# A smaller arena request for the second key tile, a product kept in SBUF, both root spreads ahead of the output, and layer 0's squares in PSUM

## The chip, the cores and the metric

The kernel runs on one core of a Trainium2 chip. The core has five engines with a queue of instructions each, all in order: TensorE (PE; its weight loads are listed as PEld), VectorE (DVE), ScalarE (ACT), GpSimd (POOL) and SyncE (SP), which issues most of the transfers. They wait for one another through semaphores. SBUF is the working memory, 128 partitions wide; PSUM, which TensorE writes to, has eight banks of 512 float32 columns. The metric is the device time of one execution in microseconds, lower is better, compared by medians of several runs.

## What is computed

A decoder trunk of two layers on 512 tokens of width 1024. Each layer normalizes x, projects it for four token mixers (retention, a convolution, a gated DeltaNet and HGRN2), projects their outputs back, and adds a SwiGLU feed-forward part. A last normalization ends it.

```python
D_MODEL, SEQ, DEPTH, D_GROUP, HEAD_DIM, N_HEADS, D_FF = 1024, 512, 2, 256, 64, 4, 2816

for l in range(DEPTH):
    h = rms_norm(x, norm_mix_w[l])
    proj = h @ w_in[l]                                  # 3592 columns
    (rq, rk, rv, rg, ca, cg, gq, gk, gv, gg, gb, ga, hq, hf, hi, hgate) = split(proj)
    ret = head_group_norm(retention_mixer(rq, rk, rv), ret_norm_w[l]) * silu(rg)   # rq, rk are rotated
    conf = conformer_conv_mixer(ca, cg, ...)            # GLU, 31 causal taps, layer norm, swish
    gdn = head_rms_norm(gated_deltanet_mixer(gq, gk, gv, gb, ga, ...), ...) * silu(gg)
    hg = head_rms_norm(hgrn2_mixer(hq, hf, hi, ...), ...) * silu(hgate)
    x = x + concat([ret, conf, gdn, hg]) @ w_out[l]
    h = rms_norm(x, norm_ffn_w[l])
    x = x + (silu(h @ ffn_w_gate[l]) * (h @ ffn_w_up[l])) @ ffn_w_down[l]
return rms_norm(x, final_norm_w)

def rms_norm(x, w, eps=1e-6):
    return x * rsqrt(mean(x * x, axis=-1) + eps) * w
```

## The kernel before

**Layout and number format.** x is kept transposed: eight tiles `x[k]` of 128 channels by 512 tokens. Every float32 operand of a large product is split into a rounded part and the rest (`xh`, `xl`; `whi`, `wlo`), and a product is three matmuls: high by high, low by high, high by low (`mm3`, L461 to L463; for token-major projections L486 to L488). The weights come by DMA into `wraw` (five buffers) and are split by ACT (the cast, L257 or L383) and POOL or DVE (the rest, L258 or L384).

**Order.** The program is written in one order, and the framework lays out each engine's queue from it: an instruction with an earlier place goes first, unless a model of the times says that its inputs or buffers aren't there yet. From then on each queue is fixed. A tile from a pool waits for the release of the buffer that it takes over. Where two instructions touch the same PSUM bank, they are ordered even if they touch different columns.

**PSUM.** The eight banks are two pools of four. `pd` takes the large projections (one bank each, two for token-major ones, `dense_t`, L486 to L488), the input `glu` of the convolution, which is read there by all its taps, and some intermediates of the weight splits. `pm` takes everything else.

**The root mean squares.** `ssq_add` squares one `x[k]` on ACT (L219 for k = 0, straight into `ssq`; L221 into a tile `sq` of a pool of two buffers) and adds it to `ssq` on DVE (L223). `rstd_sum` sums over the channels with matmuls (L231) and takes the reciprocal root on POOL (L213); `rstd_spread` spreads it over the partitions with matmuls (L242) into a `pm` bank, which ACT copies to `rsb` (L246). At the start of layer 0, `split_x` (L251 on ACT, L252 on DVE) and the squares run while x is still arriving, beside POOL's first weight splits.

**The mixers.** `layer` runs the projections in the list `ORDER` (.., ca1, cg1, hgate, rk0, rk1, rq0, rq1, rv, rg). After each projection its evicting function `ev[..]` is emitted. The mixers `gdn`, `hgrn`, `conf` and `ret` are generators; `tick()` moves each active one a step on, after every two slices of a projection. Their SBUF tiles come from an arena of 43 units (`Arena`; tiles of 2 or 4 units, the eight x tiles serve as spare ones of 2). Before an eviction, `ar.can(..)` asks whether the tiles listed in `NEED` for the first two letters of the projection's name can be had; while not, the mixers are ticked. A rotary projection (`ev_rot`) takes two tables `cosr` and `sinr` with rk0 alone (made on POOL, L722 and L723), and two tiles `sw` and `raw` with each of rk0, rk1, rq0 and rq1: ACT copies the swapped halves to `sw` (L727, L728), DVE multiplies the bank by the cosine into `raw` (L729), POOL multiplies `sw` by the sine and adds it (L730, L731). The convolution `conf_taps` runs twice, for two halves of the channels: a first tap (L1288), 23 taps on DVE (L1292), seven on ACT and POOL (L1296, L1298), and a sum (L1302), after which two of its three tiles go back to the arena.

**The feed-forward part.** Beyond its first four columns of tiles it multiplies by a scheme of seven half-width products for each pair (`step`, names e, t1, t2, g, h, t3, t4). It has two banks: `ab` and `cd`, each with a lower and an upper half (`LO`, `UP`) of 256 columns. It is called 26 times per layer, 52 in all. The fourth-named sum is completed late: `end`, with product t4, is put on the list `last`, and runs within the next `step` after its t1. Before the change ACT copies e from cd (L1648), t1 from ab's upper half into cd's upper half (L1650), t2 (L1653) and t3 (L1659, to the tile `u3`); DVE adds the first two sums (L1656) and t3 to cd's upper half (L1660).

**The end.** The last two row tiles of the second layer's down projection are done by token halves. `leave(half)` then spreads the roots of one half, multiplies the eight x tiles by them (k = 1, 4, 7 on POOL from `rsb`, L1696; the others on DVE from the bank, L1698), and issues the output transfers (L1699), even k from ACT's queue, odd k from SP's.

Of the kernel before, what the change touches and what calls it, by code (L numbers as in the profile page):

```python
# [138 lines left out]
def kernel(  # L139
# [72 lines left out]

        GP.tensor_tensor(y, a, mhalf[:, :n], op=ALU.pow)  # L213

    def ssq_add(k, keep=False, c=slice(0, T)):

        sq = sqp.tile([P, T], F32, name="sq")
        if k == 0:
            S.activation(ssq[:, c], x[k][:, c], AF.Square)  # L219
        else:  # L220
            S.activation(sq[:, c], x[k][:, c], AF.Square)  # L221
            if not keep:
                V.tensor_tensor(ssq[:, c], ssq[:, c], sq[:, c], op=ADD)  # L223
        return sq
# [13 lines left out]
    def rstd_spread(blocks=range(NB), half=True):  # L238

        pb = pm.tile([P, T], F32, name="pm")  # L240
        for b in blocks:
            PE.matmul(pb[:, b * P:(b + 1) * P], rst[:, b:b + 1].broadcast_to([P, P]), ident, start=True, stop=True)  # L242
        if half:
            V.tensor_scalar(rsh, rst, 0.5, None, op0=MUL)
        c = slice(blocks[0] * P, (blocks[-1] + 1) * P)
        S.copy(rsb[:, c], pb[:, c])  # L246
        return pb
# [362 lines left out]
    def layer(l, ar, ga, open_mix, gvp, gzp):  # L610
# [796 lines left out]
        def ret_blocks(rk, rq, v, kT, og, pt, scores):  # L1407
            S0 = None
            for b in range(NB):
# [31 lines left out]
                if b % 2 == 1:  # L1441
# [5 lines left out]

        after = {max(("gg", "gv1"), key=ORDER.index): ("gdn", gdn), "hi": ("hgrn", hgrn), "cg1": ("conf", conf), "rv": ("ret", ret)}
        NEED = dict(gg=(4,), hi=(4,), hg=(4,), rv=(4,), rg=(4,), hf=(4, 4, 2, 2), hq=(4,), ca=(2,), cg=(2, 2),
                    rk=(2, 2, 2, 2), rq=(2, 2))  # L1450
        pend = []
        for n, nm in enumerate(ORDER):
            if nm == "gg":
                while not ar.can(*NEED[nm]):
                    tick()
                for ps in dense_t_wide(G + 2 * H):
                    ev_gg(ps)
                continue
            elif nm in T_GROUPS:
                ps = dense_t(G)  # L1460
            elif l == 0 and n < 2:
                if n == 0:
                    first = dense_c2()
                ps = first[n]
            else:

                ps = dense_c(xh, xl, range(KD), pm.tile([P, T], F32, name="pm") if n < 2 else None)
            pend.append((nm, ps))
            if n == R_SUM[l]:
                rstd_sum(range(NB), ssq)  # L1470
            if n < R_SUM[l] + 1:
                continue
            if n == R_SUM[l] + 1:
                rstd_spread()
            for nm, ps in pend:
                while not ar.can(*NEED.get(nm[:2], ())):
                    tick()
                ev[nm](ps)
                if nm in after:
                    q, f = after[nm]  # L1480
                    start(l, q, f())
            pend = []


    for k in range(KD):
        ssq_add(k)
    with tc.tile_pool(name="mload", bufs=1) as mlp:
        mf = mlp.tile([P, 7 * HD], F32, name="mf")
        nc.sync.dma_start(mf, msk)
# [2 lines left out]
    for l in range(DEPTH):  # L1492
# [47 lines left out]
        with tc.tile_pool(name=f"ffp{l}", bufs=1, reuse_waits="tile") as ffp, \  # L1540
# [95 lines left out]
            def step(of, first, second):  # L1636

                def product(ps, nm, start=False):
                    hi, lo = w_next()
                    for k in range(KD // 2):  # L1640
                        mm3(ps, hi, lo, k, *of(k, nm), start and k == 0, k == KD // 2 - 1, True)

                ab = pm.tile([P, T], F32, name="pm")
                cd = pm.tile([P, T], F32, name="pm")
                gs = fft.tile([P, T], F32, name="gs")
                u3 = fft.tile([P, HC], F32, name="u3")
                product(cd[:, LO], "e", True)
                S.copy(gs[:, LO], cd[:, LO])  # L1648
                product(ab[:, UP], "t1", True)
                S.copy(cd[:, UP], ab[:, UP])  # L1650
                finish()
                product(cd[:, LO], "t2")
                S.copy(gs[:, UP], cd[:, LO])  # L1653
                product(ab[:, LO], "g")
                product(ab[:, UP], "h")
                V.tensor_tensor(ab, ab, gs, op=ADD)  # L1656
                first(ab)
                product(cd[:, LO], "t3")
                S.copy(u3, cd[:, LO])  # L1659
                V.tensor_tensor(cd[:, UP], cd[:, UP], u3, op=ADD)  # L1660

                def end():
                    product(cd[:, LO], "t4")
                    second(cd)
                last.append(end)
# [21 lines left out]

                    last.append(lambda: hidden_split(HEAD + PART * (part + 1)))

            def leave(half):  # L1690

                c = slice(half * T // 2, (half + 1) * T // 2)
                pb = rstd_spread(range(2 * half, 2 * half + 2), False)
                for k in range(KD):
                    if k % 3 == 1:
                        GP.tensor_tensor(x[k][:, c], x[k][:, c], rsb[:, c], op=MUL)  # L1696
                    else:
                        V.tensor_tensor(x[k][:, c], x[k][:, c], pb[:, c], op=MUL)  # L1698
                    (nc.sync if k % 2 else nc.scalar).dma_start(out[k * P:(k + 1) * P, c], x[k][:, c])  # L1699

            def down_plain(rows):
                order = plain_order(l, rows)
# [35 lines left out]
            if l + 1 == DEPTH:  # L1738

                rstd_sum(range(NB // 2, NB), ssq, sq)  # L1740
                leave(0)
                leave(1)


def pack(inputs):
# [81 lines left out]
```

## Time and profile before

| what | value |
|---|---|
| median of 3 runs | 1335.5 us (1333.13 to 1335.95) |
| the profiled execution | 1333.43 us |
| its span, first to last instruction | 1331.6 us |
| mean granted TensorE clock | 0.978 |
| weight loads busy (PEld) | 1177.3 us |
| moved by DMA | 124.52 MB, 94 GB/s in the mean |

The profile is of one execution on the chip. Busy times count an engine's instructions, not its waits. A row of a timeline gives start, duration, engine, line, operation, output <- inputs, shapes and count; in brackets how long the engine had been idle before and what it waited for. A row of groups gives the count, the busy time in all and the mean in ns of one, then the idle time before them and what ended it. The granted clock is the share of TensorE's full clock that the throttle let through.

### The profile page before, as it was taken

The numbers are of one execution on the slowest core, as the hardware profiler recorded it, in microseconds if no ns is written. First come the engines' busy times: TensorE is split into PE (matmuls) and PEld (weight loads), VectorE is DVE, ScalarE is ACT, GpSimd is POOL, SyncE is SP. The second block draws the span as 40 slices with busy tenths as digits, with TensorE's granted clock in tenths as the row PEclk, the third lists the DMA queues.
The fourth block names the chain that finished last, engine by engine and source line by source line (L and its number), as shares of the span: only waits on it lengthen the run. The fifth ranks groups of instructions, "written<-read, shape, count | busy, mean of one in ns | idle before, by whom it ended". The sixth has DMA issues, their size and how long they took to land.

```text
span 1331.6 us, 23717 instructions
## 1 busy us (share of the span) xinstructions
PE 1287.8 (97%) x8984; PEld 1177.3 (88%) x8984; DVE 897.5 (67%) x1569; ACT 705.5 (53%) x1454; POOL 788.4 (59%) x669
## 2 busy tenths in 40 slices
PE   8999998899999999999999999999999999999996
PEld 6888887888889999999888889889788999999995
DVE  5753778646787867876465448686559777678645
ACT  5553543535456656655545435445444665566554
POOL 6376773753255765676545767747523666566762
PEclk9999998899999999999999999889999999999998
DMA  7223210134043333342542232002423243333322
GB/s 270 79 79 105 75 25 9 41 111 134 25 135 96 111 112 96 97 126 80 164 138 80 81 88 67 25 1 71 154 69 103 80 123 102 110 97 110 122 78 72
DMA packets 60386, 124.52 MB, mean 94 GB/s; under 512 B 17520, under 2 KB 26992, under 8 KB 60272
## 3 DMA queue, kind: packets, MB, share of 16 engines
q1 hardware_dynamic: 58832, 121.83, 30.0%
q8 instruction: 71, 1.16, 0.4%
q10 hardware_dynamic: 1440, 1.18, 0.3%
q14 instruction: 43, 0.35, 0.1%
HBM read 116.17 MB, written 6.82 MB: 92 GB/s over the span
## 4 chain that ended last, share of the span: by engine, by line
PE 82%; DVE 8%; POOL 5%; ACT 3%; issue 2%; DMA 0%; SPq 0%; POOLq 0%; ACTq 0%; DVEq 0%
PE pm L461 12%; PE pm L462 12%; PE pm L463 12%; PE pd L461 10%; PE pd L462 10%; PE pd L463 10%; PE pd L486 2%; PE pm L1189 2%; PE pd L488 2%; PE pd L487 2%; POOL wlo L258 2%; DVE x L1292 1%; PE pm L928 1%; ACT whi L383 1%; PE pm L1062 1%
## 5 line engine op out<-in xcount | busy, mean ns | idle before, releaser
L258 POOL TENSOR_TENSOR wlo<-wraw,whi 128x512 fp32r<-128x512 f32 (+2 forms) x192 | 248.9, 1305 | 227.3 <-ACT whi L257 186.7
L384 POOL TENSOR_TENSOR wlo<-wraw,whi 128x512 fp32r<-128x512 f32 x208 | 272.5, 1329 | 104.4 <-ACT whi L383 99.9
L461 PE MATMUL pm<-bh,whi 128*128 128x256 f32 x1008 | 282.5, 282 | 3.9 <-ACT pm L1650 2.0
L462 PE MATMUL pm<-bl,whi 128*128 128x256 f32 x1008 | 281.2, 280 | 0.0
L463 PE MATMUL pm<-bh,wlo 128*128 128x256 f32 x1008 | 276.5, 280 | 0.0
L257 ACT CAST whi<-wraw 128x512 fp32r<-128x512 f32 (+2 forms) x212 | 125.3, 598 | 188.1 <-PE pd L462 105.1
L461 PEld LDWEIGHTS pm<-bh,whi 128*128 128x128 f32 x1008 | 189.6, 188 | 6.8 <-DVE pm L1660 3.1
L462 PEld LDWEIGHTS pm<-bl,whi 128*128 128x128 f32 x1008 | 190.0, 188 | 0.5
L463 PEld LDWEIGHTS pm<-bh,wlo 128*128 128x128 f32 x1008 | 187.8, 189 | 0.1
L383 ACT CAST whi<-wraw 128x512 fp32r<-128x512 f32 x208 | 126.7, 624 | 50.1 <-PE pm L462 42.7
L461 PE MATMUL pd<-xh,whi 128*128 128x512 f32 x384 | 151.6, 396 | 0.6 <-DVE x L729 0.6
L463 PE MATMUL pd<-xh,wlo 128*128 128x512 f32 x384 | 151.9, 396 | 0.0
L462 PE MATMUL pd<-xl,whi 128*128 128x512 f32 x384 | 151.6, 396 | 0.0
L384 DVE TENSOR_TENSOR wlo<-pd,whi 128x512 fp32r<-128x512 f32 x156 | 107.3, 688 | 52.4 <-ACT whi L383 49.9
L383 ACT CAST whi<-pd 128x512 fp32r<-128x512 f32 x156 | 92.0, 590 | 64.9 <-PE pm L462 22.6
L378 POOL TENSOR_TENSOR wraw<-wraw 128x512 f32<-128x512 f32 x52 | 68.8, 1324 | 78.2 <-DVE pd L366 65.9
L486 PE MATMUL pd<-whi,xh 128*128 128x256 f32 (+1 forms) x320 | 94.2, 295 | 8.0 <-DVE x L1292 3.4
L487 PE MATMUL pd<-wlo,xh 128*128 128x256 f32 (+1 forms) x320 | 93.7, 293 | 0.0
L488 PE MATMUL pd<-whi,xl 128*128 128x256 f32 (+1 forms) x320 | 93.5, 293 | 0.0
L461 PEld LDWEIGHTS pd<-xh,whi 128*128 128x128 f32 x384 | 72.3, 188 | 16.7 <-DVE x L729 0.8
L462 PEld LDWEIGHTS pd<-xl,whi 128*128 128x128 f32 x384 | 72.2, 188 | 16.0
L463 PEld LDWEIGHTS pd<-xh,wlo 128*128 128x128 f32 x384 | 72.2, 188 | 15.9
(359 smaller groups left out, 3181.0 us busy)
## 6 DMA issues: line engine op xcount, KB each, us to landing
wraw<-in_wf_dram SPq DMA_DIRECT2D x88, 512.0 KB, 3.6
wraw<-in_wc_dram SPq DMA_DIRECT2D x34, 512.0 KB, 3.6
wraw<-in_wd_dram SPq DMA_DIRECT2D x32, 512.0 KB, 4.0
wraw<-in_wt_dram SPq DMA_DIRECT2D x16, 512.0 KB, 3.6
wraw<-in_wo_dram SPq DMA_DIRECT2D x32, 256.0 KB, 2.6
x<-in_xt_dram SPq DMA_DIRECT2D x16, 256.0 KB, 3.7
wraw<-in_wd_dram SPq DMA_DIRECT2D x16, 256.0 KB, 2.7
wraw<-in_wd_dram SPq DMA_DIRECT2D x20, 128.0 KB, 2.0
```

The lines of the kernel that those rows point to most:

```text
L257: S.copy(hi[:, :n], r)
L258: eng.tensor_tensor(lo[:, :n], r, hi[:, :n].bitcast(F32), op=SUB)
L378: GP.tensor_tensor(src, c, a, op=SUB)
L383: S.copy(hi, src)
L384: eng.tensor_tensor(lo, src, hi.bitcast(F32), op=SUB)
L461: PE.matmul(ps, hi[:, w], ah, start=first, stop=False, skip_group_check=shared)
L462: PE.matmul(ps, hi[:, w], al, start=False, stop=False, skip_group_check=shared)
L463: PE.matmul(ps, lo[:, w], ah, start=False, stop=last, skip_group_check=shared)
L486: PE.matmul(o, xh[k][:, tk], hi[:, w], start=(k == 0 and first), stop=False)
L487: PE.matmul(o, xh[k][:, tk], lo[:, w], start=False, stop=False)
L488: PE.matmul(o, xl[k][:, tk], hi[:, w], start=False, stop=(k == KD - 1 and last))
L1189: PE.matmul(ps[:, (bb * 2 + ct) * P:(bb * 2 + ct + 1) * P], k[:, ct * T + b * P:ct * T + (b + 1) * P], qx[:, (ct * NB + b) * P:(ct * NB + ...
```

## The change

There are four edits. In `NEED`, the second key tile rk1 gets an entry of its own, which asks for two tiles of 2 units instead of four. In `step`, ACT copies t1 to an SBUF tile `p5` instead of cd's upper half; cd's upper half is then written once, as the sum of t3, read from cd's lower half, and `p5`; the copy L1659 goes. `leave` spreads both halves' roots before any multiplication, and multiplies the last tile of the second half on DVE instead of POOL. In layer 0's first seven additions of squares, the square goes to a `pd` bank instead of the SBUF tile.

```diff
--- before.py
+++ after.py
@@ -212,9 +212,9 @@
 
         GP.tensor_tensor(y, a, mhalf[:, :n], op=ALU.pow)
 
-    def ssq_add(k, keep=False, c=slice(0, T)):
-
-        sq = sqp.tile([P, T], F32, name="sq")
+    def ssq_add(k, keep=False, c=slice(0, T), bank=False):
+
+        sq = (pd.tile([P, T], F32, name="pd") if bank else sqp.tile([P, T], F32, name="sq")) if k or not bank else None
         if k == 0:
             S.activation(ssq[:, c], x[k][:, c], AF.Square)
         else:
@@ -1447,7 +1447,7 @@
 
         after = {max(("gg", "gv1"), key=ORDER.index): ("gdn", gdn), "hi": ("hgrn", hgrn), "cg1": ("conf", conf), "rv": ("ret", ret)}
         NEED = dict(gg=(4,), hi=(4,), hg=(4,), rv=(4,), rg=(4,), hf=(4, 4, 2, 2), hq=(4,), ca=(2,), cg=(2, 2),
-                    rk=(2, 2, 2, 2), rq=(2, 2))
+                    rk=(2, 2, 2, 2), rk1=(2, 2), rq=(2, 2))
         pend = []
         for n, nm in enumerate(ORDER):
             if nm == "gg":
@@ -1473,7 +1473,7 @@
             if n == R_SUM[l] + 1:
                 rstd_spread()
             for nm, ps in pend:
-                while not ar.can(*NEED.get(nm[:2], ())):
+                while not ar.can(*NEED.get(nm, NEED.get(nm[:2], ()))):
                     tick()
                 ev[nm](ps)
                 if nm in after:
@@ -1483,7 +1483,7 @@
 
 
     for k in range(KD):
-        ssq_add(k)
+        ssq_add(k, bank=True)
     with tc.tile_pool(name="mload", bufs=1) as mlp:
         mf = mlp.tile([P, 7 * HD], F32, name="mf")
         nc.sync.dma_start(mf, msk)
@@ -1643,11 +1643,11 @@
                 ab = pm.tile([P, T], F32, name="pm")
                 cd = pm.tile([P, T], F32, name="pm")
                 gs = fft.tile([P, T], F32, name="gs")
-                u3 = fft.tile([P, HC], F32, name="u3")
+                p5 = fft.tile([P, HC], F32, name="u3")
                 product(cd[:, LO], "e", True)
                 S.copy(gs[:, LO], cd[:, LO])
                 product(ab[:, UP], "t1", True)
-                S.copy(cd[:, UP], ab[:, UP])
+                S.copy(p5, ab[:, UP])
                 finish()
                 product(cd[:, LO], "t2")
                 S.copy(gs[:, UP], cd[:, LO])
@@ -1656,8 +1656,7 @@
                 V.tensor_tensor(ab, ab, gs, op=ADD)
                 first(ab)
                 product(cd[:, LO], "t3")
-                S.copy(u3, cd[:, LO])
-                V.tensor_tensor(cd[:, UP], cd[:, UP], u3, op=ADD)
+                V.tensor_tensor(cd[:, UP], cd[:, LO], p5, op=ADD)
 
                 def end():
                     product(cd[:, LO], "t4")
@@ -1687,16 +1686,17 @@
 
                     last.append(lambda: hidden_split(HEAD + PART * (part + 1)))
 
-            def leave(half):
-
-                c = slice(half * T // 2, (half + 1) * T // 2)
-                pb = rstd_spread(range(2 * half, 2 * half + 2), False)
-                for k in range(KD):
-                    if k % 3 == 1:
-                        GP.tensor_tensor(x[k][:, c], x[k][:, c], rsb[:, c], op=MUL)
-                    else:
-                        V.tensor_tensor(x[k][:, c], x[k][:, c], pb[:, c], op=MUL)
-                    (nc.sync if k % 2 else nc.scalar).dma_start(out[k * P:(k + 1) * P, c], x[k][:, c])
+            def leave():
+
+                pbs = [rstd_spread(range(2 * half, 2 * half + 2), False) for half in range(2)]
+                for half, pb in enumerate(pbs):
+                    c = slice(half * T // 2, (half + 1) * T // 2)
+                    for k in range(KD):
+                        if k % 3 == 1 and (half == 0 or k < KD - 1):
+                            GP.tensor_tensor(x[k][:, c], x[k][:, c], rsb[:, c], op=MUL)
+                        else:
+                            V.tensor_tensor(x[k][:, c], x[k][:, c], pb[:, c], op=MUL)
+                        (nc.sync if k % 2 else nc.scalar).dma_start(out[k * P:(k + 1) * P, c], x[k][:, c])
 
             def down_plain(rows):
                 order = plain_order(l, rows)
@@ -1738,8 +1738,7 @@
             if l + 1 == DEPTH:
 
                 rstd_sum(range(NB // 2, NB), ssq, sq)
-                leave(0)
-                leave(1)
+                leave()
 
 
 def pack(inputs):
```

## The prediction

> **What bounds the kernel now.** First the totals, then stretches of the execution by engine. The columns of a stretch: length, busy time (instructions) of PE, weight loads, DVE, ACT and POOL, granted TensorE clock, DMA share, GB/s.
>
> ```profile
> span 1331.6 us, 23717 instructions
> PE 1287.8 (97%) x8984; PEld 1177.3 (88%) x8984; DVE 897.5 (67%) x1569; ACT 705.5 (53%) x1454; POOL 788.4 (59%) x669
> ...
> 0.00:30.00 30.00, 26.18 (x88) 19.04 (x89) 19.88 (x28) 17.33 (x32) 19.98 (x25) 0.94 0.82 297
> ...
> 450.00:480.00 30.00, 29.91 (x253) 29.71 (x252) 22.43 (x37) 17.44 (x38) 20.11 (x16) 1.00 0.32 103
> ...
> 237.00:266.00 29.00, 28.97 (x225) 28.87 (x227) 18.66 (x31) 16.64 (x32) 24.77 (x25) 0.90 0.15 47
> 200.50:237.00 36.50, 28.19 (x239) 25.54 (x236) 29.94 (x62) 13.44 (x29) 12.55 (x10) 0.89 0.03 8
> 852.90:889.20 36.30, 31.60 (x239) 29.27 (x236) 30.34 (x61) 13.02 (x28) 12.38 (x10) 0.76 0.03 8
> ```
>
> TensorE is the bound: 97% busy, 1331.6 - 1287.8 = 43.8 us idle. Only an edit that removes PE idle time, or lets PE run at a better clock, can move the end. In the feed-forward part (450 to 480) PE idles 0.1 us and the clock is 1.00; 253 matmuls, nearly all of 256 columns, take 29.9 us, so 0.118 us each. The mixers lose far more: between 200.5 and 237 PE idles 36.5 - 28.2 = 8.3 us, and the same place of layer 1 (852.9 to 889.2) idles 4.7 us, both at a lowered clock (0.89, 0.76). These two stretches hold only small matmuls, because no projection can start there. The timelines of the single engines say why (start, us, engine, line, op, out<-in, [idle before <- releaser]):
>
> ```profile
> 176.57 0.58 ACT L727 COPY x<-pd 32x512 f32<-32x512 f32 x1
> ...
> 189.97 1.27 POOL L722 TENSOR_TENSOR x<-cs,rsb 128x512 f32<-128x512 f32 x1
> ...
> 191.71 0.68 DVE L729 TENSOR_TENSOR x<-pd,x 128x512 f32<-128x512 f32 x1
> ...
> 192.82 0.48 PE L461 MATMUL pd<-xh,whi 128*128 128x512 f32 x1
> ...
> 200.14 0.39 PE L463 MATMUL pd<-xh,wlo 128*128 128x512 f32 x1
> ...
> 196.25 0.81 DVE L1288 TENSOR_SCALAR x<-pd,hcw,vc 128x512 f32<-128x512 f32 x1 [2.44 <-POOL x L731]
> ...
> 236.99 0.69 DVE L1302 TENSOR_TENSOR x<-x,x 128x511 f32<-128x511 f32 x1
> 237.72 0.69 DVE L729 TENSOR_TENSOR x<-pd,x 128x512 f32<-128x512 f32 x1
> ...
> 237.03 0.55 PE L486 MATMUL pd<-whi,xh 128*128 128x256 f32 x1 [3.40 <-DVE x L1292]
> ```
>
> L729 is the product that empties a rotary projection's PSUM bank. rk0's runs at 191.71 and hands its bank to rq1's product (192.82 to 200.14). rk1's, whose copies ran from 176.57, comes only at 237.72, right behind L1302, the last step of the convolution's second half (begun at 196.25). Until then the four "pd" banks hold rk1, rq0, rq1 and the convolution's input, and PE's next projection (rv) starts at 237.03 after a wait of 3.40.
>
> **The keys' request.** I followed the arena's lists through the emission order by hand. When rk1 comes, 40 of 43 units are out and one tile of 2 is free. The old request of four tiles needs 40 + 3 x 2 = 46: refused. So the mixers are ticked until the convolution's second half has been emitted and returns two tiles (five ticks), and rk1's product then lands in one of these: that is why L729 follows L1302. The new request of two needs 40 + 2 = 42: granted at once, in a fresh tile. rk1's L729 then waits for its copies (done by about 179) and the cosine table (189.97 + 1.27 = 191.2), and can run behind rk0's, at about 192.4. One bank is free 45 us earlier.
>
> The refusal doesn't vanish: it moves to rq0, where 42 + 2 = 44 is over 43. So rq0 and rq1 keep their banks until 237, as does the convolution's input. What one bank allows is half of rv: 8 slices x 2 token blocks x 3 matmuls = 48 at 0.118 = 5.7 us, which can stand in the idle 8.3 us of layer 0 and in the 4.7 us of layer 1. From 237 to 266 PE is 28.97 of 29 us busy, so what was done before shortens that. The ret mixer starts when rv is out, so it moves along. In the queues: DVE takes rk1's 0.7 us ahead of the convolution's 41 us, and POOL an L731 (1.3 us); both only change places. ACT and POOL must split rv's weights earlier, and POOL is busy 12.55 of 36.5 us there. SP's weight loads follow the splits, in a stretch with a DMA share of 0.03.
>
> Upper end per layer: 5.7, and if the filler also lifts the clock from 0.89 to 1.00, 28.2 x 0.11 = 3.1 more: 9. Lower end: nothing excludes a loss, because all following instructions change places in queues that run in order; the unit of such a loss is the 3.40 us wait above. I take 4 per layer (most of 5.7, since a gap can be too short for a matmul triple): **8 us**, with ends -7 and +18.
>
> **The fifth product.** The same matmul line and two helpers, kept apart by shape, and then two of its stalls:
>
> ```profile
> L461 PE MATMUL pm<-bh,whi 128*128 128x256 f32 x1008 | 282.5, 282 | 3.9 <-ACT pm L1650 2.0 <-DVE pm L1660 1.9
> L461 PEld LDWEIGHTS pm<-bh,whi 128*128 128x128 f32 x1008 | 189.6, 188 | 6.8 <-DVE pm L1660 3.1 <-ACT pm L1650 2.8
> L1659 ACT COPY u<-pm 128x256 f32<-128x256 f32 x52 | 19.3, 371 | 12.4 <-PE pm L463 12.0
> L1650 ACT COPY pm<-pm 128x256 f32<-128x256 f32 x52 | 19.3, 371 | 4.5 <-PE pm L463 4.0
> ...
> 415.89 0.28 PE L463 MATMUL pm<-bh,wlo 128*128 128x256 f32 x1
> ...
> 416.26 0.36 ACT L1650 COPY pm<-pm 128x256 f32<-128x256 f32 x1 [0.20 <-PE pm L463]
> ...
> 416.67 0.39 PE L461 MATMUL pm<-bh,whi 128*128 128x256 f32 x1 [0.50 <-ACT pm L1650]
> ...
> 395.96 0.43 DVE L1660 TENSOR_TENSOR pm<-pm,u 128x256 f32<-128x256 f32 x1 [0.62 <-ACT u L1659]
> ...
> 396.45 0.39 PE L461 MATMUL pm<-bh,whi 128*128 128x256 f32 x1 [0.23 <-DVE pm L1660]
> ```
>
> At 415.89 "t1" ends; the next product, "t2", writes the lower half of the bank cd, and waits because L1650 writes the upper half of that bank. With the copy in an SBUF tile, cd isn't touched, and the wait goes. What is late next: "g" and "h" write the bank that the copy reads, but "t2" (12 x 0.118 = 1.4 us) stands before them and the copy takes 0.37. At 396.45 "t4" waits for the sum L1660, and that for the copy L1659 (0.37 us). Without this copy the sum starts that much sooner and the 0.23 to 0.4 us stalls go. The sum keeps its shape (one PSUM and one SBUF input), so I leave it at 0.43. ACT loses 52 x 0.371 = 19.3 us, which is worth nothing by itself: ACT is busy 53%. The new tile lives two products longer, in two buffers, and a step takes seven products. PE idle 3.9 and weight-load idle 6.8 are the ends of what the stalls cost (a stall shows in either). That they would reappear as waits for weights is possible, so the low end is 0. I take **4.5**.
>
> The Trainium skill speaks against this edit: "Perfetto Trace Analysis", section "Optimizing Scalar/DVE Operations", gives ScalarE about 93 ns of overhead on SBUF against about 51 on PSUM, and by that the t1 copy would take 42 ns more, 2.2 us of ACT in all. The rows disagree: 371 ns into PSUM and 371 into SBUF. By either, ACT has the room.
>
> **The squares.** Sums over DVE rows with both inputs in SBUF (L223) and with one in PSUM (L1714), and the first microseconds:
>
> ```profile
> L223 DVE TENSOR_TENSOR ssq<-ssq,sq 128x512 f32<-128x512 f32 x33 | 32.1, 972 | 0.8 <-ACT sq L221 0.5
> L1714 DVE TENSOR_TENSOR x<-x,pd 128x512 f32<-128x512 f32 x30 | 19.7, 677 | 2.3 <-PE pd L463 2.3
> ...
> 10.34 4.99 POOL L258 TENSOR_TENSOR wlo<-wraw,whi 128x512 fp32r<-128x512 f32 x3 [4.82 <-ACT whi L257]
> ...
> 11.34 1.15 DVE L223 TENSOR_TENSOR ssq<-ssq,sq 128x512 f32<-128x512 f32 x1 [0.54 <-ACT sq L221]
> 12.42 1.75 DVE L252 SCALAR_TENSOR_TENSOR xl<-x,vc,xh 128x512 fp32r<-128x512 f32 x1
> 14.10 1.78 DVE L223 TENSOR_TENSOR ssq<-ssq,sq 128x512 f32<-128x512 f32 x1
> ...
> 20.72 3.47 DVE L223 TENSOR_TENSOR ssq<-ssq,sq 128x512 f32<-128x512 f32 x2
> ...
> 14.23 0.77 PE L462 MATMUL pm<-xl,whi 128*128 128x512 f32 x1 [1.75 <-DVE xl L252]
> ...
> 34.42 1.05 PE L242 MATMUL pm<-cs,rst 128*128 128x128 f32 x8
> ...
> PE pd L486 <- DVE z L674: 2.6, 1, 2.6
> ```
>
> An addition from PSUM takes 677 ns whatever POOL does; one from SBUF alone is stretched to 1.15 to 1.78 while POOL's splits run. The four stretched ones give back 1.15 + 1.78 + 3.47 - 4 x 0.68 = 3.7 us of DVE. The first, at 11.34, stands before the xl on which PE waits 1.75 us: xl could start 0.4 to 0.5 sooner. If it then also ran unstretched (0.75), PE would get 1.4. The Trainium skill's rule limits this: "SBUF — State Buffer", section "Who interferes with whom", has a DVE instruction with two SBUF inputs and a GpSimd read block each other for whole instructions, and xl keeps two, so by it xl still stands out POOL's split, and the gain is about 0.5. I take 0.5 from the start difference alone. Four banks instead of two buffers also end ACT's waits for L223.
>
> A sum that is ready earlier can bring the whole root earlier: spread at 34.42, evictions after it, and at their end PE's 2.6 us wait for z. But PE's place for the spread is fixed when the program is laid out, so from 0 to 2.6; I take 1. The seven squares leave their banks by 24 us, before gg needs them. Together **1.5**, ends 0 and 3.1.
>
> **The end.** ACT's queue and stretches of the last microseconds:
>
> ```profile
> 1321.26 0.37 ACT L246 COPY rsb<-pm 128x256 f32<-128x256 f32 x1 [0.71 <-PE pm L242]
> 1322.12 1.87 ACTq L1699 DMA_DIRECT2D out_dram<-x  x4
> 1324.03 0.37 ACT L246 COPY rsb<-pm 128x256 f32<-128x256 f32 x1 [2.40 <-POOL x L1696]
> ...
> 1324.00:1326.00 2.00, 0.00 (x0) 0.00 (x0) 1.57 (x5) 0.37 (x1) 1.52 (x3) 0.50 1.05 335
> 1326.00:1328.00 2.00, 0.00 (x0) 0.00 (x0) 0.17 (x1) 0.00 (x0) 0.57 (x1) 0.50 0.82 269
> ```
>
> The second copy of the roots stands in ACT's queue behind four output DMAs. Moved ahead of them it runs at about 1323 instead of 1324.03, and the second half's products follow. But the output is bound by its DMAs (335 GB/s, share 1.05), and only the dip to 269 can be won: (1 - 269/335) x 2 = 0.4 us. Against it, ACT's first output DMA now waits for the second copy, about 1 us. **0**, ends -0.9 and +0.4.
>
> **Sum.** 8 + 4.5 + 1.5 + 0 = 14. The profiled execution took 1333.4 (its span 1331.6 and 1.8 around it), 2.1 under the median of 1335.5. 1333.4 - 14 = 1319.4, 1335.5 - 14 = 1321.5; I forecast 1321.
>
> **Rivals.** (A) The wait only moves on: rq0 takes the keys' place, rv's half isn't put forward in PE's order, or what is won before 237 is lost behind 266, where the output projection waits for ret. For: the count above. Against: rq1 did use rk0's bank 0.4 us after it was free. Only 4.5 + 1.5 remain: 1329.5. Chance 0.18. (B) More than half of rv: the freed bank is used again by rg, and the clock recovers: 18 + 6.8 + 3.1 = 28, so 1308. Chance 0.13. (C) Slower: rv's early matmuls stand in PE's queue before the DeltaNet's and wait there for a weight split or the second bank, and each such stop holds a chain that feeds DVE, whose convolution steps free the banks. A stop costs about 3.4 us, as at 237.03. With 6 us won elsewhere it decides from two stops in all; four give 1335.5 - 6 + 13.6 = 1343. Against it: rq1's 24 matmuls ran in that place without one. Chance 0.19, of which 0.12 end slower. The forecast itself has 0.50 (1313 to 1328).
>
> A measurement of this kernel tells some 0.2% (2.7 us) from no change. Faster: 0.50 + 0.13 + 0.15 of A = 0.78; the same: 0.03 of A and 0.07 of C; slower: 0.12. From 1309 to 1337 leaves out half of B and the slow part of C.
>
> **What would show it.** Keys: L729 twice near 192, L486 matmuls on pd between 200 and 237, and PE idle there under 5 us. Fifth: no PE wait on the t1 copy and under 1 us on the sum. Squares: every L223 of the first 25 us near 0.68. End: both copies L246 before 1324, counted from the same point. Wrong would be: pd matmuls still beginning at 237, or new PE waits between 190 and 300.

## The result, and the profile after

| kernel | median, us | runs | ratio to before, 95% interval |
|---|---|---|---|
| before | 1335.07 | 1333.13 to 1335.95 | |
| after | 1305.09 | 1303.31 to 1307.05 | 0.9778 [0.9756, 0.9799] |
| after, measured again beside its variants | 1305.36 | 1302.63 to 1307.67 | 0.9789 [0.9763, 0.9814] |

The forecast was 1321, with a range from 1309. The change took 30.0 us off (1335.07 - 1305.09), where the sum of the terms was 14. The page of the kernel after, its totals and its groups:

```profile
span 1300.1 us, 23700 instructions
...
PE 1268.8 (98%) x8984; PEld 1162.2 (89%) x8984; DVE 883.4 (68%) x1570; ACT 690.8 (53%) x1402; POOL 788.1 (61%) x668
...
L461 PE MATMUL pm<-bh,whi 128*128 128x256 f32 x1008 | 281.1, 281 | 0.0
...
L461 PE MATMUL pd<-xh,whi 128*128 128x512 f32 x384 | 153.2, 400 | 4.3 <-DVE ar L637 4.3
```

Three things are to be seen here. First, the same 8984 matmuls are busy for 1268.8 us instead of 1287.8: 19.0 us less for the same work. Second, PE's idle time fell from 43.8 to 31.3 (1300.1 - 1268.8), 12.5 us. So more than half of the gain is not idle time. Third, the feed-forward matmuls no longer wait (3.9 before, 0.0 now), while a wait of 4.3 us on L637 is new.

The keys, in the timeline of DVE and then of PE, kernel after:

```profile
192.54 0.69 DVE L729 TENSOR_TENSOR x<-pd,x 128x512 f32<-128x512 f32 x1 [1.55 <-POOL x L722]
193.15 0.68 DVE L729 TENSOR_TENSOR ar<-pd,x 128x512 f32<-128x512 f32 x1
...
236.34 0.69 DVE L1302 TENSOR_TENSOR x<-x,x 128x511 f32<-128x511 f32 x1
237.06 0.69 DVE L729 TENSOR_TENSOR x<-pd,x 128x512 f32<-128x512 f32 x1
```

```profile
30.73 1.05 PE L242 MATMUL pm<-cs,rst 128*128 128x128 f32 x8
...
204.00 0.28 PE L486 MATMUL pd<-whi,xh 128*128 128x256 f32 x1
...
214.07 0.28 PE L486 MATMUL pd<-whi,xh 128*128 128x256 f32 x1
236.29 0.38 PE L486 MATMUL pd<-whi,xh 128*128 128x256 f32 x1 [0.26 <-DVE x L1292]
```

Both keys' products run at 192.5 and 193.2; rq0's follows L1302, as the count of the arena had it. Sixteen L486 matmuls, a third of the 48 that make half of rv, run between 204.0 and 214.1, and the next one comes at 236.29. The first row also shows the root's spread 3.7 us earlier than in the kernel before (34.42 to 30.73); how much of this the squares make is taken up below. The stretches of the kernel after that answer to those of the prediction (same columns):

```profile
0.00:30.00 30.00, 26.17 (x97) 19.23 (x98) 14.43 (x28) 17.74 (x33) 19.99 (x26) 0.94 0.83 298
200.50:237.00 36.50, 34.64 (x340) 31.80 (x338) 32.59 (x65) 17.30 (x39) 16.61 (x13) 1.00 0.05 15
237.00:266.00 29.00, 28.70 (x235) 27.20 (x233) 21.03 (x41) 15.77 (x31) 27.78 (x30) 1.00 0.20 65
```

Between 200.5 and 237 PE now idles 1.9 us instead of 8.3, and the granted clock, 0.89 and 0.90 before in the last two stretches, is 1.00 in both. In the first 30 us DVE is busy 14.43 us instead of 19.88. Of these 5.4 us, 3.6 are the seven additions of squares (8.3 us before, 4.7 now) and 1.4 the xl tiles, L252 (7.9 and 6.5). The view of groups by shape has the seven in one row:

```profile
L223 DVE TENSOR_TENSOR ssq<-ssq,pd 128x512 f32<-128x512 f32 x7 | 4.7, 678 | 0.0
```

To see where the gain arises I divided each profiled execution at the first matmul of each root mean square (L231); the differences of these starts are the lengths, in us. The two columns in the middle are kernels of the next section, with the keys' edit alone and with all edits but the squares:

| stretch | before | keys alone | all but the squares | after |
|---|---|---|---|---|
| start to the first root | 25.9 | 24.2 | 24.1 | 22.0 |
| layer 0, mixers | 309.5 | 296.2 | 296.2 | 303.3 |
| layer 0, feed-forward | 342.9 | 343.0 | 337.5 | 337.5 |
| layer 1, mixers | 306.9 | 301.0 | 299.9 | 297.0 |
| layer 1, feed-forward | 333.7 | 333.7 | 328.7 | 328.7 |
| last root to the end | 12.7 | 11.6 | 11.6 | 11.6 |
| span | 1331.6 | 1309.7 | 1298.0 | 1300.1 |

Each column is one execution. The first stretch differs by some 2 us between kernels that are equal up to there (24.0 in one of them). The mixers differ too where the code is the same: over four kernels without the keys and the squares, layer 0 took 309.5 to 312.5 us and layer 1 306.0 to 309.4. So differences of 2 to 3 us in these rows are not read.

### The profile page after: what moved, and what is told of

It reads as the page before. It is cut to its first block, busy times and chain, and to the rows that moved or that the text cites. A ratio compares the mean times of both kernels' runs of the same rounds, so it can differ in the third digit from the quotient of the medians.

```text
span 1300.1 us, 23700 instructions
## 1 busy us (share of the span) xinstructions
PE 1268.8 (98%) x8984; PEld 1162.2 (89%) x8984; DVE 883.4 (68%) x1570; ACT 690.8 (53%) x1402; POOL 788.1 (61%) x668
## 4 chain that ended last, share of the span: by engine, by line
PE 91%; DVE 6%; POOL 1%; ACT 1%; DMA 1%; issue 0%; SPq 0%; DVEq 0%; POOLq 0%; ACTq 0%
PE pm L461 14%; PE pm L462 14%; PE pm L463 14%; PE pd L461 11%; PE pd L463 11%; PE pd L462 11%; PE pd L486 3%; PE pd L488 3%; PE pd L487 3%; PE pm L1189 2%; DVE x L1292 1%; PE pm L928 1%; DVE ar L623 1%; DVE ar L1197 1%; PE pm L1051 1%; PE pm L1036 1%
## 5 line engine op out<-in xcount | busy, mean ns | idle before, releaser
L486 PE MATMUL pd<-whi,xh 128*128 128x256 f32 (+1 forms) x320 | 92.5, 290 | 5.6 <-DVE z L674 3.4
L463 PEld LDWEIGHTS pd<-xh,wlo 128*128 128x128 f32 x384 | 72.7, 189 | 16.3
```

Source lines behind the costliest of these rows:

```text
L463: PE.matmul(ps, lo[:, w], ah, start=False, stop=last, skip_group_check=shared)
L486: PE.matmul(o, xh[k][:, tk], hi[:, w], start=(k == 0 and first), stop=False)
```

## The experiments

### Each edit by itself

Four kernels, each with one edit on the kernel before. **The keys** (one_keys):

```diff
-                    rk=(2, 2, 2, 2), rq=(2, 2))
+                    rk=(2, 2, 2, 2), rk1=(2, 2), rq=(2, 2))
...
-                while not ar.can(*NEED.get(nm[:2], ())):
+                while not ar.can(*NEED.get(nm, NEED.get(nm[:2], ()))):
```

> The kernel before with the keys' entry in NEED alone. Theory 1 (each edit acts at its own place; the sizes are those read from the two traces): some 20 us faster, 10 in each layer's mixer, near 1315. Theory 2 (the sizes forecast): 8 us faster, near 1327. Theory 3 (the edits help one another, the keys' entry needs the others): under 4 us faster.

1312.74 us (1309.57 to 1314.07), ratio 0.9843 [0.9819, 0.9867]: 20.9 us of 1332.65, where my term was 8. The stretch from rq1's first matmul to rg's last holds the same work in both kernels (in layer 0 524 matmuls, in layer 1 521), so it can be compared directly. First two stretches of the kernel before, then the same of the kernel with the keys alone, layer 0 and layer 1:

```profile
192.80:265.40 72.60, 64.26 (x524) 60.08 (x522) 53.46 (x97) 32.68 (x65) 42.77 (x42) 0.91 0.07 23
845.10:915.00 69.90, 65.14 (x521) 61.21 (x521) 52.50 (x97) 32.46 (x65) 42.38 (x40) 0.88 0.07 21
```

```profile
191.10:252.60 61.50, 57.72 (x524) 54.08 (x522) 49.58 (x97) 32.42 (x65) 42.40 (x41) 1.00 0.08 27
833.10:895.10 62.00, 57.39 (x521) 54.04 (x522) 50.69 (x96) 32.10 (x66) 41.74 (x39) 1.00 0.08 24
```

Layer 0 is shorter by 11.1 us: idle time fell from 72.60 - 64.26 = 8.34 to 3.78, which is 4.6, and the busy time of the same 524 matmuls by 6.5, with the clock up from 0.91 to 1.00. Layer 1 is shorter by 7.9, of which 0.15 is idle time (4.76 to 4.61) and 7.75 is busy time (0.88 to 1.00). The gain is 19.0 us here, and 14.3 of it is busy time. Finer windows show that this is the clock: in the kernel before it is 0.50 for 13.7 us of the first stretch and 17.1 us of the second, in which PE is busy for 12.8 and 16.3 us. At full clock half of that would go, 14.6 us. With the keys alone the clock is 1.00 through both stretches. The rest of one_keys' 21.9 us of span adds up from smaller stretches of both signs: 1.7 at the start, 2.2 and 0.9 behind rg, 1.1 at the end, and 2.9 lost in layer 1 ahead of rq1.

**The fifth product** (one_fifth):

```diff
-                u3 = fft.tile([P, HC], F32, name="u3")
+                p5 = fft.tile([P, HC], F32, name="u3")
...
-                S.copy(cd[:, UP], ab[:, UP])
+                S.copy(p5, ab[:, UP])
...
-                S.copy(u3, cd[:, LO])
-                V.tensor_tensor(cd[:, UP], cd[:, UP], u3, op=ADD)
+                V.tensor_tensor(cd[:, UP], cd[:, LO], p5, op=ADD)
```

> The kernel before with the product kept in SBUF and summed from the bank, alone. Theory 1: 10.4 us faster (5.4 in layer 0's feed-forward part, 5.0 in layer 1's), near 1325. Theory 2 (the forecast size): 4.5 us faster. Theory 3: under 4 us.

1321.83 us (1318.30 to 1326.26), ratio 0.9916 [0.9886, 0.9947], 11.2 us; my term was 4.5. The two feed-forward parts of the kernel before, then of one_fifth:

```profile
335.40:678.30 342.90, 339.69 (x2539) 322.76 (x2537) 251.03 (x412) 202.28 (x427) 205.27 (x162) 1.00 0.35 108
985.20:1318.90 333.70, 330.37 (x2525) 316.47 (x2524) 242.02 (x410) 198.93 (x422) 191.75 (x151) 1.00 0.31 94
```

```profile
336.50:674.00 337.50, 337.50 (x2540) 322.53 (x2538) 249.25 (x412) 195.52 (x401) 210.75 (x162) 1.00 0.36 109
983.30:1312.40 329.10, 329.08 (x2526) 316.88 (x2525) 241.88 (x410) 191.76 (x396) 191.57 (x151) 1.00 0.32 95
```

They are shorter by 5.4 and 4.6 us, 10.0 in all. Idle time gives 3.2 + 3.3 = 6.5 of it; the other 3.5 us is busy time at a clock of 1.00 throughout. A stop costs more than its wait, and this is about the size of it. In the prediction's row at 416.67 the first matmul after a wait of 0.50 lasts 0.39 instead of 0.28, and the timeline of PE in the kernel before shows the next one:

```profile
416.90 0.28 PE L462 MATMUL pm<-bl,whi 128*128 128x256 f32 x1
417.01 0.28 PE L463 MATMUL pm<-bh,wlo 128*128 128x256 f32 x1
```

From the last start before the stop (415.89) to 416.90 there are 1.01 us in place of two steps of 0.118: 0.77 lost, where the idle time says 0.50. The list of PE's waits in layer 0's feed-forward part of the kernel before (us in all, times, longest) counts the stops:

```profile
PE pd L461 <- ACT ph L1568: 1.2, 1, 1.2
PE pm L461 <- ACT pm L1650: 1.0, 2, 0.5
PE pm L461 <- DVE pm L1660: 0.9, 3, 0.3
```

Six stops in each layer, twelve in all, at 0.27 more (0.77 - 0.50) make 3.2, near the 3.5. This is an estimate from one stop.

**The squares** (one_squares; `bank=True`, the first and the fourth hunk of the change) and **the end** (one_end; the last two hunks):

```diff
-        sq = sqp.tile([P, T], F32, name="sq")
+        sq = (pd.tile([P, T], F32, name="pd") if bank else sqp.tile([P, T], F32, name="sq")) if k or not bank else None
...
-        ssq_add(k)
+        ssq_add(k, bank=True)
```

> The kernel before with layer 0's squares in PSUM alone. Theory 1: the spread of the roots comes 3.7 us sooner, 1.4 of it is left at 53 us, and the end is 0 to 1.5 us sooner. Theory 2 (the forecast): 1.5 us faster. Theory 3: the early change shifts the whole layer 0 mixer, and the time moves by 3 us or more either way.

```diff
-                leave(0)
-                leave(1)
+                leave()
```

> The kernel before with both roots spread ahead of the products, alone. Theory 1: 1.1 us faster, all after the last projection. Theory 2 (the forecast): no change. What counts is the stretch from the last projection's end to the end of the span.

The squares by themselves: 1332.63 us in ten runs, ratio 0.9995 [0.9973, 1.0018], no difference that can be told. Its profiled execution was the slowest of the ten. In it the first root came at 21.2, against 24.0 to 25.9 in kernels without the edit, and the mixers of layer 0 took 316.9 against 309.5 to 312.5. So something is gained and given back; that is taken up below. The end: 1332.86 us in ten runs, 0.9989 [0.9969, 1.0009]. Its last stretch is 11.7 instead of 12.7, but it is 11.6 with the keys alone, where that edit is absent. So the end has no gain that these runs show.

### Is it the bank, or the order of emission?

The smaller request changes two things: rk1's bank is freed, and the convolution's steps are emitted five ticks later against rk1's eviction. keys_fresh keeps the old request with its five ticks and gives rk1's product a tile of its own:

```diff
-                sw, raw = ar.get(2), ar.get(2)
+                sw = ar.get(2)
+                raw = ar.fresh(2) if (nm, ct) == ("rk", 1) else ar.get(2)
```

> The kernel before, old request, so the five ticks stay, and with them the order in which everything is emitted; but rk1's raw tile is a fresh one (two units over the arena's count), so its product no longer waits for the convolution's end. Theory 1 (the gain comes from the PSUM bank that rk1's product frees): rk1's L729 near 192, 48 matmuls of rv ahead of the convolution's end, and most of the 20 us. Rival (the gain comes from the order: mixers five steps behind the projections): under 5 us, L729 may be early all the same.

1313.81 us (1308.85 to 1316.32), ratio 0.9844 [0.9811, 0.9877], equal to one_keys (0.9843). rk1's product runs at 190.80, behind rk0's at 190.19. The bank that is free earlier is the cause. It is not the ticks.

### Is it the clock?

warm8 adds 112 needless matmuls of 256 columns to the kernel before, in the second half of the convolution of both layers; nothing reads their results. The bank isn't freed earlier than before (rk1's product runs at 243.2; 237.7 before).

```diff
                 if n % CONF_TAPS == CONF_TAPS - 1:
+                    if ct == 1:
+                        pw = pm.tile([P, T], F32, name="pm")
+                        for _ in range(8):
+                            PE.matmul(pw[:, :G], xh[0][:, :P], xl[0][:, :G], start=True, stop=True)
                     yield
```

> The kernel before with 7 times 8 needless matmuls of 256 columns in each second half of the convolution (112 in all; by 0.118 us 13 us of PE work, with nobody reading them). Theory 1 (part of the gain is the granted clock, which PE's idle time between 200 and 237 lowers to 0.89 and 0.76): the clock there rises towards 1.00 and the time doesn't rise, it falls by up to 6 us. Rival (only the useful work that is put forward counts): the clock rises or not, the time stays or rises by up to 13 us.

1327.02 us in nine runs, ratio 0.9952 [0.9936, 0.9968]: 6.4 us faster with more work. One stretch of the kernel before, and the same of warm8:

```profile
190.00:270.00 80.00, 71.40 (x577) 66.66 (x576) 59.51 (x109) 35.63 (x71) 50.00 (x51) 0.91 0.09 27
```

```profile
190.00:270.00 80.00, 75.53 (x651) 70.99 (x652) 60.87 (x113) 37.54 (x74) 51.01 (x50) 0.98 0.09 28
```

In the same 80 us warm8 issues 74 matmuls more, and the clock is 0.98. Over the whole execution PE does 112 matmuls more and is busy 3.7 us less (1287.8 and 1284.1). This profile is of the fastest of the nine runs, but the mean clock is 0.986 to 0.990 in all nine, against 0.976 to 0.981 in the fourteen runs of the kernel before beside them. The new instructions could also have helped by shifting the queues. So the same matmuls were put into a kernel in which that stretch is filled already: all edits but the squares (no_squares, below), with a clock of 1.00 from 180 to 240.

> The 112 needless matmuls of warm8 (in the second half of the convolution of both layers), now put into the kernel without the squares in PSUM, where rv's first half already fills that stretch and the granted clock from 180 to 240 is 1.00. Theory: warm8 gained 0.0048 because the needless matmuls kept the granted clock up where TensorE idled; here nothing is left to recover, so there is no gain, and up to 112 x 0.118 = 13 us of work that now finds little idle time costs something: ratio 0.976 to 0.985, 1302 to 1315. Rival: warm8 gained because the additional instructions changed the order of the queues; then a gain of some 6 us can come here too: 0.971, 1296.

1308.23 us (1306.64 to 1308.85), ratio 0.9807 [0.9790, 0.9823], against 0.9759 [0.9737, 0.9782] without them: there the same work costs 6.4 us (0.0048 of 1334). The mean clock stays where it was (0.991 to 0.993, against 0.989 to 0.994), and PE is busy 13.4 us more (1265.3 and 1278.7), which is the price of 112 matmuls at 0.118 us. Where the clock had dropped, needless matmuls gained; where it hadn't, they cost. The order of the queues also differs between these kernels and may have a share in the 6.4 us of warm8. But that the clock makes up most of the keys' gain is shown by this and by the busy time of the same matmuls above.

### Which copy held the feed-forward part?

t1_sbuf moves only the copy of t1 to SBUF; ACT still copies t3, into a tile of a new pool `ffu` that has one buffer where `u3` had two.

```diff
-                u3 = fft.tile([P, HC], F32, name="u3")
+                p5 = fft.tile([P, HC], F32, name="p5")
+                u3 = ffu.tile([P, HC], F32, name="u3")
...
-                S.copy(cd[:, UP], ab[:, UP])
+                S.copy(p5, ab[:, UP])
...
-                V.tensor_tensor(cd[:, UP], cd[:, UP], u3, op=ADD)
+                V.tensor_tensor(cd[:, UP], p5, u3, op=ADD)
```

> The kernel before with t1 copied to SBUF, but t3 still copied by ACT before the sum. Theory 1: the gaps before t2 go (6.4 us with the slower first matmul after each), those before t4 stay (about 1.3 us), and so does the wait at the end of each feed-forward part (2.7 us): 6 to 7 us faster. Rival (the copy of t3 is what matters, it holds ACT's queue at each step): under 3 us faster.

1326.56 us (1324.80 to 1330.87), ratio 0.9942 [0.9918, 0.9965]. Its two feed-forward parts:

```profile
335.60:676.30 340.70, 339.36 (x2538) 322.71 (x2537) 268.32 (x412) 202.03 (x427) 208.66 (x162) 1.00 0.36 108
982.40:1314.40 332.00, 330.89 (x2525) 317.24 (x2524) 258.29 (x410) 199.60 (x422) 200.59 (x151) 1.00 0.32 94
```

2.2 + 1.7 = 3.9 of the 10.0 us is here. The waits for t1's copy are gone, those for the sum remain (idle 1.34 + 1.11). The wait of 1.2 us for L1568 at the end of each part, which I expected to stay, is gone too. The sum reads both inputs from SBUF here and takes 1.02 us in the mean instead of 0.43, so DVE is busy 17 us longer per layer (251.03 to 268.32). The slower sum and the single buffer may hold back part of what t1's copy is worth, so the other 6.1 us is an upper estimate for dropping the copy of t3. Dropping that copy alone was not tried.

### Where the squares' gain goes

In the kernel after, DVE and then PE near the new 4.3 us wait:

```profile
169.94 0.77 DVE L637 SCALAR_TENSOR_TENSOR ar<-ar,pd 128x256 f32<-128x256 f32 x2
...
171.60 1.27 DVE L1197 COPY_PREDICATED ar<-mk,pm 128x512 f32<-128x512 uint8 x1
172.67 1.20 DVE L1203 TENSOR_TENSOR ar<-ar,ar 128x512 f32<-128x512 f32 x1
173.79 0.41 DVE L637 SCALAR_TENSOR_TENSOR ar<-ar,pd 128x256 f32<-128x256 f32 x1
...
175.09 0.40 DVE L637 SCALAR_TENSOR_TENSOR ar<-ar,pd 128x256 f32<-128x256 f32 x1
```

```profile
174.25 0.80 PE L461 MATMUL pd<-xh,whi 128*128 128x512 f32 x1 [4.29 <-DVE ar L637]
```

The kernel with the squares alone has the same wait, in PE's timeline:

```profile
176.54 0.79 PE L461 MATMUL pd<-xh,whi 128*128 128x512 f32 x1 [4.29 <-DVE ar L637]
```

The same place in the kernel before, DVE:

```profile
169.05 1.69 DVE L1203 TENSOR_TENSOR ar<-ar,ar 128x512 f32<-128x512 f32 x1
171.34 0.41 DVE L637 SCALAR_TENSOR_TENSOR ar<-ar,pd 128x256 f32<-128x256 f32 x1
171.80 0.40 DVE L637 SCALAR_TENSOR_TENSOR ar<-ar,pd 128x256 f32<-128x256 f32 x1
...
173.09 0.73 DVE L637 SCALAR_TENSOR_TENSOR ar<-ar,pd 128x256 f32<-128x256 f32 x2
```

L637 empties the gate projection's banks, four times. Before, the four stand close together. With the squares in PSUM the order laid out for DVE is another one, 140 us further on: mixer steps (L1197, L1203 among them) stand between the second eviction and the third, and others before the fourth. The third now comes 3.9 us after the first (173.79 - 169.94) instead of 1.8, the fourth 5.2 instead of about 2.1, and PE's next projection starts when the third is done (174.20). Three kernels test this, with the change itself beside them:

No_squares has the three other edits:

```diff
-        ssq_add(k, bank=True)
+        ssq_add(k)
```

> The change without the squares in PSUM (the other three edits as they are). Theory: the squares brought the roots some 4 us forward, but the whole and more is given back, since the laid-out order of VectorE then spreads the four gate evictions L637 near 170 between steps of the convolution, and TensorE waits 4.3 us for the third of them and runs at a granted clock near half for the next 5 us. Without the squares that wait is absent, the granted clock from 170 to 180 is 1.00, and the time is 1299 to 1303 (below the change's 1305). Rival: the squares' gain is real in this company, and without them the time is 1307 to 1309. Second rival: no difference, 1305.

Sq_pm puts the seven squares into banks of the other pool:

```diff
-        sq = (pd.tile([P, T], F32, name="pd") if bank else sqp.tile([P, T], F32, name="sq")) if k or not bank else None
+        sq = (pm.tile([P, T], F32, name="pm") if bank else sqp.tile([P, T], F32, name="sq")) if k or not bank else None
```

> The change, with the seven squares in banks of the other PSUM pool, pm. Theory: a square in any bank shortens its addition to 0.68 us, so the spread L242 stays near 31; but in this kernel's VectorE queue the four evictions L637 near 170 stand close together again, so the 4.3 us wait goes and the early start is kept: 1297 to 1302, the fastest so far. Rival: the loss in layer 0's mixer comes from the early start itself and not from the evictions' place, then the first matmul of the feed-forward part stays 294 us behind the first root matmul, or more, and the time is 1304 to 1307.

Sq_first puts only the first three there, in pd:

```diff
-        ssq_add(k, bank=True)
+        ssq_add(k, bank=k < 4)
```

> The change, with only the first three squares (those whose additions POOL stretched most) in pd banks, the other four in SBUF as before. Theory: the evictions L637 near 170 stand close together in VectorE's queue here, so no TensorE wait of over 1 us on them; most of the early start is kept: 1298 to 1303. Rival (the early start itself costs): 1304 to 1307.

And the change as it is:

> The change itself, on the same chip as the three others: 1303 to 1307, with the 4.3 us TensorE wait on L637 near 170.

| kernel | median of 5, us | ratio, interval | first spread L242 | layer 0, mixers | layer 1, mixers |
|---|---|---|---|---|---|
| no_squares | 1301.81 | 0.9759 [0.9737, 0.9782] | 32.7 | 296.2 | 299.9 |
| sq_pm | 1302.24 | 0.9767 [0.9744, 0.9789] | 34.6 | 296.1 | 303.0 |
| sq_first | 1303.56 | 0.9775 [0.9753, 0.9797] | 33.8 | 294.4 | 301.3 |
| after_again | 1305.36 | 0.9789 [0.9763, 0.9814] | 30.8 | 303.4 | 297.0 |

Wait and half clock are both seen in short stretches of the kernel after, and are absent in no_squares (second fence):

```profile
170.00:175.00 5.00, 0.75 (x2) 0.66 (x3) 5.00 (x10) 2.07 (x4) 1.76 (x2) 0.80 0.40 56
175.00:180.00 5.00, 5.00 (x14) 3.94 (x13) 1.62 (x4) 1.21 (x2) 4.55 (x4) 0.52 0.00 0
```

```profile
170.00:175.00 5.00, 5.00 (x33) 4.48 (x33) 4.84 (x13) 3.22 (x7) 2.11 (x3) 1.00 0.00 0
175.00:180.00 5.00, 5.00 (x31) 4.38 (x31) 3.91 (x5) 3.77 (x7) 2.36 (x2) 1.00 0.47 66
```

In all three variants the evictions stand close together again, the wait is absent, and the mixers of layer 0 take 294.4 to 296.2 instead of 303.4: some 7 us are lost there, about what the wait of 4.3 us and the half clock around its end make together (6.8 us, see the last section, in which PE is busy for 5.6 us, so 2.8 us of work is lost). This part of the theory held. Two things went against my expectations. sq_pm and sq_first lost the early start: their L242 at 34.6 and 33.8 is no earlier than in kernels without the edit (32.4 to 34.5), while the kernels with all seven squares in `pd` have it at 30.0 to 30.8. Neither became faster than no_squares. And layer 1, whose squares none of them touches, is 3 to 6 us shorter in the change: 297.0 against 299.9 to 303.0. Some 3 us of that can be the spread between executions; what the rest is stays open.

No_squares has the lowest median of the study, though it can't be told from sq_pm. Against after_again, the means of five runs each are 1301.6 and 1305.0; worked out from the spread of these runs, the difference is 3.3 us with a 95% interval of about 0.9 to 5.8. So three of the four edits, without the squares, are a little better than the change.

## Why the prediction fell short

**For the keys and the fifth product the direction and the mechanism were right and the sizes wrong; the squares' gain didn't come.** The forecast sum had 14 us. The single edits measured 20.9, 11.2, 0.7 and 1.5 us, of which the last two can't be told from nothing. Together the four give 30.0, some 4 less than these added up; the squares' loss in company, 3.3 us, is near that.

**Keys: 8 taken, 20.9 measured; this is the step that failed.** What would show it came as written: L729 twice near 192, L486 in between, 1.9 us of idle time there. The idle time that was won in layer 0, 4.6 us, is near the 4 that I took; in layer 1, where I took 4 as well, it was 0.15, and nearly the whole gain there was busy time. What failed is the sentence "Upper end per layer: 5.7, and if the filler also lifts the clock from 0.89 to 1.00, 28.2 x 0.11 = 3.1 more: 9", and that the clock then went into the upper end alone. Three quarters of what came in the two stretches was clock (14.3 of 19.0 us). And the rows that the prediction quotes already held its size: beside 28.19 busy us at 0.89 they show 28.97 at 0.90 right behind, and 31.60 at 0.76 in layer 1. Worked out in the same way for all three rows, 28.19 x 0.11 + 28.97 x 0.10 + 31.60 x 0.24 = 3.1 + 2.9 + 7.6 = 13.6 us, against 14.3 measured in the two stretches, within which these rows lie but for 0.6 us. I priced one row of three. With 13.6 + 4 to 5 of idle time the term would have been 18, the end of the range that I gave to it and the place where rival B stood.

**Fifth: 4.5 taken, 10.0 measured in the two parts (11.2 by the ratio).** Both waits went as described, and the sum of t3 and the t1 tile kept its duration. Two terms were missing. The ends were the idle times of rows of groups, 3.9 and 6.8, and left out what a stop costs beside its wait: some 0.27 us each, 3.5 in all. So the premise that only idle time and the clock can move the end was too narrow: these 3.5 us were neither. And the wait for L1568 that closes each feed-forward part (1.2 us, twice) was not priced; it was an effect of the same copies, since it went with them.

**Squares: 1.5 taken, no difference that can be told alone, and 3.3 lost in company.** The additions fell to 678 ns in the mean, as said. PE's longest wait for an xl fell to 0.7 us, from 1.3 to 1.8 in the kernels without the edit, and the spread came some 2 to 4 us earlier. So the early gain was there. The step that failed is that it would last to the end: with the squares in PSUM the framework lays out the queues of the next 300 us in another order, and the wait for L637 that comes with it takes back what was won, and in company more. "New PE waits between 190 and 300" was in the list of what would show me wrong; it came at 170.

**End: 0 taken, and 0 it is.** The timeline of ACT in the kernel after:

```profile
1290.85 0.37 ACT L246 COPY rsb<-pm 128x256 f32<-128x256 f32 x1 [0.71 <-PE pm L242]
1291.70 0.35 ACTq L1699 DMA_DIRECT2D out_dram<-x  x1
1292.10 0.37 ACT L246 COPY rsb<-pm 128x256 f32<-128x256 f32 x1 [0.88 <-DVE x L1698]
1292.12 4.24 ACTq L1699 DMA_DIRECT2D out_dram<-x  x7
```

The second copy comes 3.6 us after the last root matmul (1288.5) instead of 5.1 (1324.03 - 1318.9). ACT's first output transfer, which I thought to be held up by 1 us, is issued 3.2 us after it in both kernels: the queue took it ahead of the copy.

**The rivals.** A (the wait only moves on) is refuted: the bank that is freed is used, 1.9 us of idle time remain. C (new stops before the DeltaNet) did not happen with the keys; the stop that did come belongs to the squares, at another place. B gave 1308 and is nearest. Its clock is what came; its second use of the bank by rg did not, since just the 48 matmuls of half of rv were put forward.

## What to carry to other kernels

Where a stretch runs at a granted clock under 1.00, price it as busy time x (1 - clock), for every stretch that the same gap disturbs, and take this for the likeliest value of an edit that fills the gap, not for its upper end; here that would have given 13.6 us where 14.3 came. Count a stop of TensorE from start to start of its matmuls: here it cost 0.77 us where the idle time showed 0.50. And a small edit at the start can change the order of the queues far behind it, here 140 us on, so compare the order of the evictions there before its gain is believed.

## What the runs showed of the hardware

**The clock falls to half in phases of 3.4 us or a multiple of it, and short gaps can be enough.** Single microseconds of the kernel before:

```profile
207.00:208.00 1.00, 0.05 (x1) 0.05 (x1) 1.00 (x3) 0.94 (x4) 0.51 (x1) 1.00 0.00 0
208.00:209.00 1.00, 1.00 (x11) 0.93 (x12) 0.96 (x2) 0.63 (x2) 0.60 (x1) 0.92 0.00 0
209.00:210.00 1.00, 1.00 (x7) 1.00 (x7) 0.10 (x1) 0.71 (x2) 0.05 (x1) 0.50 0.00 0
...
212.00:213.00 1.00, 1.00 (x9) 0.79 (x9) 1.00 (x3) 0.23 (x1) 0.00 (x0) 0.87 0.00 0
```

The clock is 0.50 from about 208.84 (0.92 is 0.16 us at half) to 212.26 (0.87 is 0.26 us): 3.4 us, in which about half of the work is lost. Read in the same way, the phases at the 3.40 us wait for rv (236.2 to 243.0) and, in the kernel after, at the 4.29 us wait for L637 (173.0 to 179.8) are twice as long, 6.8 us; each begins while PE is still waiting. In layer 1 of the kernel before one lasts 17.1 us, five times as long (857.4 to 874.4). The phases lie on one grid too: the starts at 208.84, 215.67 and 236.15 are 2 and 6 times 3.41 us apart. The Trainium skill, "TensorE: Matmul & The Clock Gate", section "What's actually happening", says that the gate watches a free-running window of about 3.4 us and halves the clock after at least one idle window. The length of the phases and the grid agree. The condition does not: in the 3.41 us before 208.84 PE idles for 0.98 us in all, 0.95 of it between 207 and 208, and that was enough. Nor is it the gap's length alone, since in the kernel with the keys alone PE idled for a whole microsecond with the clock staying at 1.00:

```profile
213.00:214.00 1.00, 0.00 (x0) 0.00 (x0) 1.00 (x3) 0.97 (x3) 0.58 (x1) 1.00 0.00 0
```

The idle time in one step of the grid doesn't decide it either: from 855.39 to 858.80 of the same kernel PE idles for 1.33 us, and the clock stays at 1.00 there and behind it. What decides is open. For the price it doesn't matter: each phase of 3.4 us in which PE has work takes about 1.7 us of it, at 208.84 more than the idle time before it.
